# A hybrid decoder step: array divisions of the RWKV recurrence, 32x32 blocks in the GLA mixer, and decode states moved in halves

## The chip, the cores and the metric

The kernel runs on one core of one Trainium2 chip. The metric is the device time of one execution in microseconds (us), as the median of three runs. One more execution was taken by the hardware profiler. Its rows are what this document reads. The engines are called as in the profile: PE (matrix multiplications), DVE, ACT and POOL (elementwise work), SP (it issues the loads). POOL also issues the stores.

## What is computed

A trunk of four layers, each a mixer followed by an MLP with squared ReLU, works on 256 prompt tokens and 8 sampled tokens (one for each of 8 decode sequences). The tokens lie side by side as 264 columns, with the 1024 features in 8 groups of 128 partitions. The mixers are RWKV-7, GLA, a short convolution and a pooling. The change touches the first two.

```python
def step(S, inp):                       # RWKV-7, 16 heads of 64 values x 64 keys
    r_t, w_t, k_t, v_t, a_t, b_t = inp
    sa = einsum('bhvk,bhk->bhv', S, a_t)
    S = S * w_t[:, :, None, :] + sa[..., None] * b_t[:, :, None, :] + v_t[..., None] * k_t[:, :, None, :]
    return S, einsum('bhvk,bhk->bhv', S, r_t)

def step(S, inp):                       # GLA, 4 heads of 128 keys x 256 values
    qc, kc, vc, gc = inp
    b = cumsum(gc, axis=1)
    o_inter = einsum('bchk,bhkv->bchv', qc * exp(b), S)
    dec = exp(where(mask, b[:, :, None] - b[:, None, :], -inf))
    att = einsum('btshk,bthk,bshk->bhts', dec, qc, kc)
    o_intra = einsum('bhts,bshv->bthv', att, vc)
...
def sqrelu_mlp(x, w_up, w_down):
    return square(relu(x @ w_up)) @ w_down
```

Both mixers also update a state for each of the 8 decode sequences (`state_rwkv_wkv`, `state_gla`), which is loaded, used once and stored.

## The kernel before

**Stages.** The program runs the RWKV mixer, MLP 0, the GLA mixer, MLP 1, the convolution, MLP 2, the pooling and MLP 3. Weights come in tiles of 512 KB by SP's queue. In the RWKV mixer they are used as float32 (`wfull`, line 272; each float32 matmul stands as two records in the trace). Elsewhere they are split into a high and a low float32r part (`whi`, `wlo`, lines 180 and 188) and used in three matmuls (lines 232 to 234).

**Divisions of the array.** A matmul with 128 rows and 128 columns of weights uses the whole array. A matmul that reads 64 or 32 partitions, or writes 64 or 32, uses a part of it, and the array is divided accordingly (128x64, 64x64, 32x32 and so on, rows x columns). The profile prints a matmul's rows and columns, as in `64*64`.

**RWKV mixer.** The prompt is cut into 4 chunks of 64 tokens. Projections (`acc<-xm,wfull`) and three low-rank paths (`ps<-lo,wa`, `ps<-hw,wa`, the gate's `ps<-lx,g1a`, `ps<-lx,g1b`) come first. `keys` normalises the keys (`pss<-ksq,ph` sums squares per head into 8 rows, `pkk<-kc,gb` spreads the result from 8 rows back over 128). `pA` forms each chunk's products. A triangular solve on DVE (`zt`, `Zs`, 124 instructions) follows, ending in two transposes, `Zt` and `Wt`. Two rounds of `pQ` (32x32 blocks) complete the inverse. Then the recurrence over the chunks runs: `state_step` does `pU`, copies it to `Us`, does `pSA<-Us,MT`, copies that to `XV`, does `pS<-XV,BT` and updates `XV`. `output_step` does `pY<-rT,XV` and `pY<-AR,XV`. In `pSA` and in the first `pY` the two heads of a pair lie on the upper and the lower 64 partitions (64x64 division). In `pU`, `pS` and the second `pY` they lie on the left and right 64 columns (128x64 division). `rT` is the receptance times the decay, and `rb` a block form of it for `pAr`. `gate` does `pg<-hg,g2a` and `pg<-hg,gb`. `dacc<-yo,wfull` (line 1053) is the output projection.

**Decode of RWKV.** `decode` updates the states `wS` in four quarters of 512 KB. Each quarter is loaded in two halves (one per 64 partitions), and after the update both halves are stored, and the tile for the quarter after the next is loaded. These steps are advanced one at a time inside MLP 0.

**GLA mixer.** A prompt tile has 128 tokens. The attention matrix is built by levels: level n covers pairs of blocks of 64, 32, ..., 1 tokens, plus the diagonal. Levels 0 and 1 are small matmuls (line 1248). Levels 2 to 7 each take 4 whole 128x128 matmuls (line 1253, `gA<-gZQ,gEX`), and a masked copy of 128x512 (COPY_PREDICATED, line 1254) picks the few blocks that count. For decode, each state half `gSs` is split into a high and a low part (`gSq`, on ACT, DVE and POOL) and multiplied in float32r (line 1410, `gos<-gSq,gqz`, 128x32 division). `decode_update` (line 1396) then forms the new state.

**Order.** `RWKV_PLAN` and `GLA_PLAN` are written by hand. Each word is one step of a named piece of work. Tables (`RWKV_ENGINES`, `GLA_ENGINES`) give each copy or product its engine (V is DVE, A is ACT, G is POOL). Each engine runs its own instructions in order.

Of the kernel before, what the change touches and what calls it, by code (L numbers as in the profile page):

```python
# [450 lines left out]
def rwkv_early(k):  # L451
# [6 lines left out]
    for x in (hw, hg1, g1b, gb):  # L458
        nc.vector.memset(x, 0.0)
# [1313 lines left out]
```

## Time and profile before

| what | value |
|---|---|
| runs | 1316.86, 1316.26, 1315.95 us; median 1316.26 us |
| profiled execution | 1313.01 us, its span 1311.2 us |
| RWKV mixer | 0 to 256 us of the span |
| MLP 0 | 256 to 460 us |
| GLA mixer | 460 to 624 us |
| the rest | 624 to 1311 us |
| PE / DVE / ACT / POOL busy | 97% / 68% / 44% / 29% |
| mean granted clock of PE | 0.99 of full speed |

The span runs from the first to the last recorded instruction. The profiled execution lies 3.25 us below the median of the runs. PEclk is the granted clock in parts of 2.4 GHz, so 0.5 means 1.2 GHz. Busy time counts an instruction's own time; matmuls overlap in the pipeline, so the time from one start to the next is shorter than the mean duration of one.

### The profile page before, as it was taken

Reading aid. Unit: us, or ns where it says so; the run is one execution under the profiler, and the core shown is the slowest. Engines: PE = TensorE matmul, PEld = TensorE weight load, DVE = VectorE, ACT = ScalarE, POOL = GpSimd, SP = SyncE. Lnnn points to the kernel's source line nnn. Section 1 sums busy time; section 2 is a strip of 40 time slices with the busy share of each in tenths; the row PEclk is TensorE's granted clock in tenths of the full one; section 3 lists DMA queues with packets and bytes.
Section 4 is the critical chain, followed back from the end, with each engine's and each line's share of the span. In section 5 each row is a group of like instructions: output and inputs, shape, how many; then the busy total and the mean of one; then the engine's idle time right before and its main releaser. Section 6 shows DMA issues by size and latency. Waiting matters only on the chain.

```text
span 1311.2 us, 25583 instructions
## 1 busy us (share of the span) xinstructions
PE 1276.8 (97%) x10318; PEld 1224.9 (93%) x10318; DVE 897.5 (68%) x1398; ACT 571.4 (44%) x949; POOL 381.3 (29%) x415
## 2 busy tenths in 40 slices
PE   8999999999899998999999999999999999999997
PEld 7888787999899987899999999999999999999996
DVE  6467978697855579988766455877665556666443
ACT  2512343543434443346545344445444445444342
POOL 6133144243300227545333000332332002233000
PEclk9999989999999999999999999999999999999998
DMA  9333110467566542644655555555655673555552
GB/s 277 103 119 107 48 51 10 137 197 196 184 209 198 168 148 87 216 170 152 187 179 176 193 177 176 181 180 163 191 177 180 206 234 97 159 180 177 185 185 83
DMA packets 168024, 211.10 MB, mean 161 GB/s; under 512 B 11569, under 2 KB 125137, under 8 KB 167906
## 3 DMA queue, kind: packets, MB, share of 16 engines
q1 hardware_dynamic: 165122, 201.82, 48.8%
q0 software_dynamic: 2784, 7.65, 1.9%
q8 instruction: 81, 1.33, 0.4%
q14 instruction: 37, 0.30, 0.1%
HBM read 200.62 MB, written 8.82 MB: 160 GB/s over the span
## 4 chain that ended last, share of the span: by engine, by line
PE 83%; DVE 10%; DMA 2%; issue 2%; ACT 1%; POOL 0%; DVEq 0%; SPq 0%; ACTq 0%; POOLq 0%
PE acc L232 11%; PE acc L234 11%; PE acc L233 11%; PE dacc L234 11%; PE dacc L233 11%; PE dacc L232 11%; PE acc L272 5%; DMA wraw<-in_ffn_up 2%; PE dacc L1053 2%; DVE wlo L188 1%; PE pss L373 1%; DVE zt L736 1%; DVE Zs L738 1%; PE pQ L761 1%; PE gE L1215 0%
## 5 line engine op out<-in xcount | busy, mean ns | idle before, releaser
L188 DVE TENSOR_TENSOR wlo<-wraw,whi 128x1024 fp32r<-128x1024 f32 x310 | 390.8, 1263 | 227.8 <-ACT whi L180 226.9
L180 ACT CAST whi<-wraw 128x1024 fp32r<-128x1024 f32 x310 | 324.4, 1049 | 405.0 <-PE dacc L233 176.8
L232 PE MATMUL acc<-xh,whi 128*128 128x264 f32 x1408 | 397.0, 286 | 3.6 <-DVE ft L399 1.6
L234 PE MATMUL acc<-xh,wlo 128*128 128x264 f32 x1408 | 398.7, 286 | 1.8 <-DVE wlo L188 1.8
L233 PE MATMUL acc<-xl,whi 128*128 128x264 f32 x1408 | 398.9, 285 | 0.0
L233 PE MATMUL dacc<-sl,whi 128*128 128x264 f32 x1024 | 288.7, 284 | 0.0
L232 PE MATMUL dacc<-sh,whi 128*128 128x264 f32 x1024 | 287.8, 284 | 0.0
L234 PE MATMUL dacc<-sh,wlo 128*128 128x264 f32 x1024 | 283.8, 284 | 0.0
L232 PEld LDWEIGHTS acc<-xh,whi 128*128 128x128 f32 x1408 | 263.5, 189 | 6.6 <-DVE ft L399 2.2
L234 PEld LDWEIGHTS acc<-xh,wlo 128*128 128x128 f32 x1408 | 264.0, 188 | 4.8 <-DVE wlo L188 2.6
L233 PEld LDWEIGHTS acc<-xl,whi 128*128 128x128 f32 x1408 | 265.0, 188 | 0.5
L403 POOL TENSOR_TENSOR fs<-ft 128x264 f32<-128x264 f32 x128 | 133.0, 1042 | 252.3 <-DVE ft L399 250.9
L233 PEld LDWEIGHTS dacc<-sl,whi 128*128 128x128 f32 x1024 | 192.8, 188 | 0.0
L232 PEld LDWEIGHTS dacc<-sh,whi 128*128 128x128 f32 x1024 | 192.6, 188 | 0.0
L234 PEld LDWEIGHTS dacc<-sh,wlo 128*128 128x128 f32 x1024 | 189.7, 188 | 0.0
L346 POOL TENSOR_TENSOR sq<-sq 128x264 f32<-128x264 f32 x35 | 32.6, 932 | 361.1 <-ACT sq L342 360.6
L272 PE MATMUL acc<-xm,wfull 128*128 128x264 f32 x384 | 89.2, 388 | 0.2
L272 PEld LDWEIGHTS acc<-xm,wfull 128*128 128x128 f32 x384 | 72.0, 190 | 14.2 <-issue 1.2
L404 DVE TENSOR_TENSOR sl<-fs,sh 128x264 fp32r<-128x264 f32 x128 | 58.2, 472 | 25.0 <-POOL fs L403 25.0
L399 DVE SCALAR_TENSOR_TENSOR ft<-acc,rstd 128x264 f32<-128x264 f32 x96 | 40.9, 428 | 38.8 <-PE acc L234 38.6
L401 ACT ACTIVATE sh<-ft 128x264 fp32r<-128x264 f32 x128 | 50.9, 420 | 37.0 <-DVE ft L399 34.8
L342 ACT ACTIVATE sq<-hT 128x264 f32<-128x264 f32 x56 | 23.5, 419 | 37.8 <-DVE hT L383 35.5
(465 smaller groups left out, 1576.7 us busy)
## 6 DMA issues: line engine op xcount, KB each, us to landing
wraw<-in_ffn_up SPq DMA_DIRECT2D x128, 512.0 KB
wraw<-in_ffn_down SPq DMA_DIRECT2D x128, 512.0 KB
wraw<-in_gla_w_in SPq DMA_DIRECT2D x24, 512.0 KB
wraw<-in_conv_w_in SPq DMA_DIRECT2D x24, 512.0 KB
wfull<-in_rwkv_wk SPq DMA_DIRECT2D x8, 512.0 KB
wfull<-in_rwkv_wv SPq DMA_DIRECT2D x8, 512.0 KB
wS<-in_state_wkv SPq DMA_DIRECT2D x16, 256.0 KB
wfull<-in_rwkv_wr SPq DMA_DIRECT2D x8, 512.0 KB
```

The costliest lines, as they stand in the source:

```text
L180: return e.copy(out, x) if scale is None else e.activation(out, x, AF.Copy, scale=scale)
L188: return self.on(site, i).tensor_tensor(out, x, y, op=op)
L232: mm(acc, h, xh, start=first, stop=False)
L233: mm(acc, h, xl, start=False, stop=False)
L234: mm(acc, l, xh, start=False, stop=last)
L272: self.nc.tensor.matmul(accs[mi][:, :NT], w[:, kk, mi * 128:(mi + 1) * 128], self.at(X, k), start=(k == 0), stop=(k == 7))
L346: self.nc.gpsimd.tensor_tensor(ss[0], ss[0], sq, op=ALU.add)
L399: nc.vector.scalar_tensor_tensor(t, acc, 0.0, rs, op0=ALU.max, op1=ALU.mult)
L401: nc.scalar.activation(h, t, AF.Square)
L403: nc.gpsimd.tensor_tensor(s, t, t, op=ALU.mult)
L404: nc.vector.tensor_tensor(l, s, h.bitcast(F32), op=ALU.subtract)
L1053: mm(acc, wo[m][:, kk, :], at(Y, kk)[:, cs], start=(kk == 0), stop=(kk == 7))
```

## The change

Four things are done, and both plans and the engine tables are written anew.

1. RWKV recurrence: `Us` becomes two tiles padded with zeros, and `output_step` uses `rb` instead of `rT`, so that `pSA` and both `pY` have 128 rows and 64 columns, and alternate the left and right half. Four `rb` tiles are kept instead of two. `keys` uses four 32-column strips for `pss` and 32 rows for `pkk`. `pQ` alternates its two halves. The gate's second part has 32 rows in strips (`g2b`). DVE's memsets of `hg1`, `g1b` and `gb` at the start go.
2. RWKV decode: the halves of a quarter are stored and loaded in separate steps.
3. GLA levels 2 to 7: 32x32 blocks on the diagonal, each a matmul of 128 rows and 32 columns of weights. Three levels share a PSUM bank, and the masked copy is 128x128, into a tile `gin` that `placed` copies to `att`.
4. GLA decode: the splits into `gSq` go. `gos` is formed in float32, with four strips of 32 columns that each hold one of the four partial sums.

```diff
-    "AAVAGAAV", "mq": "VAAAVVVA", "v": "AAVVAVAA", "vec4": "AVVVAVGV", "rb": "AGAGGVVAAAAAAGVA", "vec5": "AVVAAAAV",
+    "AAVAGAAV", "mq": "AAAAVVVA", "v": "AAVVAVAA", "vec4": "AVVVAVGV", "rb": "VVVVVVVVVVVVVVVV", "vec5": "AVVAAAAV",
...
-        p, x, c = k.bank("pss")[0:8, :NT], k.t("kx", [8, NT]), k.t("kc", [8, NT])
+        p, x, c = k.bank("pss")[:, :NT], k.t("kx"), k.t("kc")
         for mi in range(4):
-            mm(p, sel[:, mi, 0:8], sq[:, mi], start=(mi == 0), stop=(mi == 3))
+            mm(p[mi * 32:(mi + 1) * 32], k.C("rsel")[:, 0:32], sq[:, mi], start=True, stop=True)
...
-            V.tensor_tensor(r, acc[:, :NP].rearrange("p (c t) -> p c t", c=4), dc, op=ALU.mult)
...
+        for par in range(2):
+            o = OWN[par]
+            k.product("rb", m * 2 + par, rb[m // 2][o, m % 2, :, par, :], acc[o, :NP].rearrange("p (c t) -> p c t", c=4), dc[o])
...
         for qv in range(4):
             S, vs, T = wS[qv], slice(qv * 16, (qv + 1) * 16), [k.slab([128, 16, 64], "wT") for _ in range(2)]
             op(T[0], vb(vt[:, 4, vs]), kb(3), ALU.mult)
+            if qv > 0:
+                store(qv - 1, 1)
             yield
             op(T[1], vb(sav[:, vs]), kb(2), ALU.mult)
+            if qv in (1, 2):
+                decode_load(qv + 1, (0,))
             yield
...
-            for h2 in range(2):
-                k.store(Sdst[h2][:, :, qv * 1024:(qv + 1) * 1024], S[OWN[h2]].rearrange("p v k -> p (v k)"))
-            if qv < 2:
-                decode_load(qv + 2)
+            store(qv, 0)
             yield
...
-        Us = k.t("Us", [128, 256])
-        k.put("us", c * 2 + a, Us, pU[:, :256])
+        for par in range(2):
+            o = OWN[par]
+            k.put("us", (c * 2 + a) * 2 + par, Us[par][o], pU[o, :256])
...
-                mm(p[o, mi * 64:(mi + 1) * 64], MT[un // 16][o, un % 16, :], Us[o, mi * 64:(mi + 1) * 64],
-                   start=True, stop=True)
+            for par in range(2):
+                mm(p[OWN[par], mi * 64:(mi + 1) * 64], MT[un // 16][:, un % 16, :], Us[par][:, mi * 64:(mi + 1) * 64],
+                   start=True, stop=True)
...
-        for hd in range(4):
-            a, b = (EX[t][hd][:, n, :], ZQ[t][hd][:, n, :]) if n < 7 else (kT[:, hd, tok], qT[:, hd, tok])
-            mm(p[:, hd * 128:(hd + 1) * 128], a, b, start=True, stop=True)
-        V.copy_predicated(att[t][:, :, 0:128], msk[:, n, :].unsqueeze(1).to_broadcast([128, 4, 128]),
-                          p.rearrange("p (h t) -> p h t", h=4))
+        lv = range(3 * n - 4, 3 * n - 1)
+        pv = p[:, 0:384].rearrange("p (l h t) -> p l h t", l=3, h=4)
+        for i, l in enumerate(lv):
+            for hd in range(4):
+                x, y = (EX[t][hd][:, l], ZQ[t][hd][:, l]) if l < 7 else (kT[:, hd, tok], qT[:, hd, tok])
+                for j in range(4):
+                    b = slice(j * 32, (j + 1) * 32)
+                    mm(pv[b, i, hd], x[:, b], y[:, b], start=True, stop=True)
+        for i, l in enumerate(lv):
+            V.copy_predicated(inner[t], msk[:, l - 2, :].unsqueeze(1).to_broadcast([128, 4, 32]), pv[:, i])
...
-        for h2 in range(2):
-            for i in range(2):
-                met[hp] += 1
-                mm(po[hp][0:32, h2 * 256:(h2 + 1) * 256], qz[:, (hp * 2 + h2) * NS + b, :], Sp[g, h][:, i, h2, :],
-                   start=(met[hp] == 1), stop=(met[hp] == 32))
+        met[hp] += 1
+        for h in range(2):
+            for h2 in range(2):
+                r = (h2 * 2 + h) * 32
+                mm(po[hp][r:r + 32, 0:256], qz[:, (hp * 2 + h2) * NS + of(g, h)[1], :], S[g][:, h, h2, :],
+                   start=(met[hp] == 1), stop=(met[hp] == 4))
```

How the rewritten plans move instructions is seen at three places. First, the start: PE's order right behind the sums for the low-rank paths (`acc<-xg,wad`), in the kernel before. `wa` is the second low-rank weight, `g1a` and `g1b` the gate's first.

```order
L497 MATMUL acc<-xg,wad 128x264 x8
L272 MATMUL acc<-xm,wfull 128x264 x21
L617 MATMUL ps<-lx,g1a 128x264
L618 MATMUL ps<-lx,g1b 128x264
L617 MATMUL ps<-lx,g1a 128x264
```

The same place in the changed kernel.

```order
L490 MATMUL acc<-xg,wad 128x264 x8
L591 MATMUL ps<-lo_142,wa_183 128x264 x2
L613 MATMUL ps<-lx,g1a 128x264 x6
L614 MATMUL ps<-lx,g1b 128x264
L582 MATMUL ps<-hw,wa_183 128x264
L614 MATMUL ps<-lx,g1b 128x264 x4
L582 MATMUL ps<-hw,wa_183 128x264 x2
L267 MATMUL acc<-xm,wfull 128x264 x5
```

The 21 projection matmuls that stood ahead of the gate now stand behind two low-rank paths and most of the gate. SP's loads behind that, before (`wa` is loaded in two halves, `wfull` tiles are 512 KB).

```order
L150 DMA g1b<-in_rwkv_g 128x8x32
L150 DMA gb<-in_spread 16x1024
L150 DMA gb<-in_rwkv_g 32x1024
L283 DMA wfull<-in_rwkv_wk 128x4x256 x5
L150 DMA wa_189<-in_rwkv_w 64x1024
L150 DMA wa_189<-in_rwkv_a 64x1024
L283 DMA wfull<-in_rwkv_wk 128x4x256 x2
L283 DMA wfull<-in_rwkv_wv 128x4x256 x2
L150 DMA g1a<-in_rwkv_g 128x8x128
```

And in the changed kernel.

```order
L278 DMA wfull<-in_rwkv_wk 128x4x256 x7
L278 DMA wfull<-in_rwkv_wv 128x4x256
L145 DMA wa_183<-in_rwkv_w 64x1024
L145 DMA wa_183<-in_rwkv_a 64x1024
L278 DMA wfull<-in_rwkv_wv 128x4x256
L145 DMA g1a<-in_rwkv_g 128x8x128
L145 DMA g1r<-in_rwkv_g 128x8x32
```

Eight large tiles instead of five now stand ahead of `wa`, and nine ahead of `g1a`, as before. Second, DVE right behind the second transpose of the solve, before.

```order
L743 STREAM_TRANSPOSE Wt<-Zs 128x32x32
L193 TENSOR_TENSOR bg<-pb,vT 128x264
L834 SCALAR_TENSOR_TENSOR bg<-bg,prm,pg 128x264
L184 TENSOR_SCALAR gT<-pg,prm 128x264
L182 COPY MT<-Wt 32x16x32 x2
L182 COPY Qs<-pQ 32x512
L193 TENSOR_TENSOR AR<-pAr,ph 128x256 x2
L193 TENSOR_TENSOR bg<-pb,vT 128x264
L834 SCALAR_TENSOR_TENSOR bg<-bg,prm,pg 128x264 x2
```

And in the changed kernel.

```order
L738 STREAM_TRANSPOSE Wt<-Zs 128x32x32
L177 COPY MT<-Wt 32x16x32 x2
L188 TENSOR_TENSOR AR<-pAr,ph 128x256 x2
L188 TENSOR_TENSOR bg<-pb,vT 128x264
L188 TENSOR_TENSOR AR<-pAr,ph 128x256 x2
L188 TENSOR_TENSOR bg<-pb,vT 128x264
L177 COPY MT<-pQ 32x16x32 x3
L188 TENSOR_TENSOR AR<-pAr,ph 128x256 x2
L188 TENSOR_TENSOR bg<-pb,vT 128x264
L836 SCALAR_TENSOR_TENSOR bg<-bg,prm,pg 128x264 x2
```

Eight `AR` products and four `bg` products now stand behind the transpose, where there were two and two; the rest stood in the solve, among its short instructions. Third, SP in MLP 0, before (`wraw` tiles are 512 KB of weights).

```order
L221 DMA wraw<-in_ffn_up 128x4x256 x15
L150 DMA wS<-in_state_wkv 64x1x1024 x2
L221 DMA wraw<-in_ffn_up 128x4x256 x9
L150 DMA wS<-in_state_wkv 64x1x1024 x2
L221 DMA wraw<-in_ffn_up 128x4x256 x8
```

And in the changed kernel.

```order
L216 DMA wraw<-in_ffn_up 128x4x256 x19
L145 DMA wS<-in_state_wkv 64x1x1024 x2
L216 DMA wraw<-in_ffn_up 128x4x256 x8
L145 DMA wS<-in_state_wkv 64x1x1024 x2
L216 DMA wraw<-in_ffn_up 128x4x256 x5
```

The two pairs of state loads come four and three weight tiles later, and each pair still stands together.

## Rows read from the trace of the kernel before

**Rows 1.** Windows: us, busy us of each engine (instructions), granted clock, DMA.

```profile
20.00:32.00 12.00, 11.85 (x52) 9.37 (x51) 7.78 (x17) 0.94 (x2) 11.98 (x20) 1.00 1.03 286
32.00:113.00 81.00, 81.00 (x379) 66.30 (x379) 47.86 (x91) 27.19 (x73) 24.83 (x34) 1.00 0.36 115
123.00:162.00 39.00, 36.87 (x226) 31.66 (x225) 37.03 (x106) 15.85 (x44) 6.15 (x11) 0.96 0.23 68
162.00:222.00 60.00, 55.73 (x944) 46.71 (x942) 51.56 (x84) 23.99 (x55) 28.32 (x28) 0.94 0.12 33
222.00:256.00 34.00, 33.72 (x276) 32.36 (x277) 22.25 (x63) 14.62 (x41) 7.11 (x14) 1.00 0.32 98
314.00:345.00 31.00, 27.19 (x210) 25.81 (x209) 23.82 (x32) 11.59 (x17) 8.93 (x11) 1.00 0.71 186
460.00:624.00 164.00, 154.99 (x1185) 143.98 (x1184) 143.37 (x218) 74.42 (x149) 86.42 (x69) 0.99 0.48 155
```

**Rows 2.** Timeline of PE at the start: start, us, line, operation.

```profile
17.84 3.81 PE L497 MATMUL acc<-xg,wad 128*128 128x264 f32 x16
21.49 10.20 PE L272 MATMUL acc<-xm,wfull 128*128 128x264 f32 x42
31.52 0.68 PE L617 MATMUL ps<-lx,g1a 128*128 128x264 f32 x2
```

**Rows 3.** Timeline of PE, key norms: sums of squares.

```profile
92.01 1.95 PE L665 MATMUL pss<-ksq,ph 128*8 128x264 f32 x8
```

**Rows 4.** Timeline of PE, key norms: spread over the heads.

```profile
101.65 2.04 PE L675 MATMUL pkk<-kc,gb 8*128 8x264 f32 x8
```

**Rows 5.** Timeline of PE, gate and second round of 32x32 blocks.

```profile
171.94 0.61 PE L833 MATMUL pg<-hg,gb 128*128 128x264 f32 x2
172.47 3.93 PE L761 MATMUL pQ<-Wt,Qs 32*32 32x32 f32 x128
```

**Rows 6.** Timeline of PE in one step of the recurrence.

```profile
209.26 0.69 PE L990 MATMUL pU<-XV,AKa 128*64 128x64 f32 x16
...
211.03 0.22 PE L1004 MATMUL pSA<-Us,MT 64*64 64x64 f32 x1
211.04 0.22 PE L1026 MATMUL pY<-rT,XV 64*64 64x64 f32 x1
...
211.15 1.58 PE L1004 MATMUL pSA<-Us,MT 64*64 64x64 f32 x29
```

**Rows 7.** Groups of DVE in the RWKV mixer: busy us, mean ns, idle before.

```profile
L193 DVE TENSOR_TENSOR AR<-pAr,ph 128x256 f32<-128x256 f32 x16 | 6.0, 415 | 0.0
...
L834 DVE SCALAR_TENSOR_TENSOR bg<-bg,prm,pg 128x264 f32<-128x264 f32 x8 | 3.9, 483 | 3.4 <-PE pg L833 3.4
...
L786 DVE TENSOR_TENSOR rT<-acc,Dc 128x256 f32<-128x256 f32 x7 | 2.9, 419 | 0.1
...
L182 DVE COPY rb<-rT 64x256 f32<-64x256 f32 x3 | 1.0, 324 | 0.0
```

**Rows 8.** Waits in MLP 0: total us, times, longest.

```profile
ACT whi L180 <- DMA wraw<-in_ffn_up: 9.2, 3, 5.9
```

**Rows 9.** Timeline of PE in the GLA levels, with idle time and releaser.

```profile
512.26 1.95 PE L1253 MATMUL gA<-gZQ,gEX 128*128 128x128 f32 x16
...
518.66 0.68 PE L1248 MATMUL gA<-gZQ,gEX 128*64 128x64 f32 x8 [1.54 <-DVE att L1254]
```

**Rows 10.** Timeline of PE: one group of the GLA decode output.

```profile
540.16 0.62 PE L1410 MATMUL gos<-gSq,gqz 128*32 128x256 f32 x4
540.62 0.40 PE L1393 MATMUL gkv<-gvs,gkm 128*128 128x256 f32 x2
```

**Rows 11.** Groups of DVE in the GLA mixer.

```profile
L188 DVE TENSOR_TENSOR gSq<-gSs,gSq 128x512 fp32r<-128x512 f32 x9 | 10.7, 1206 | 1.1 <-ACT gSq L180 1.1
...
L1254 DVE COPY_PREDICATED att<-gmask,gA 128x512 f32<-128x512 uint32 x12 | 8.7, 734 | 2.4 <-PE gA L1253 1.4 <-ACT att L180 0.6 <-PE gA L1248 0.5
...
L182 DVE CAST gSq<-gSs 128x512 fp32r<-128x512 f32 x4 | 3.9, 966 | 0.7 <-DMA gSs<-in_state_gla 0.7
```

More of the change, by code (lines that the diff above doesn't have):

```diff
@@ L455, in rwkv_early @@
     nc = k.nc
[L457 to L460 removed]
+    hw = k.t("hw")
+    nc.vector.memset(hw[64:128], 0.0)
+    k.zeroed = hw
     st = k.res.tile([128, 8, NS], F32, name="shst")
@@ L672, in keys @@
         yield
-        for mi in range(4):
-            p = k.bank("pkk")[:, :NT]
-            mm(p, spread[0:8, mi], c, start=True, stop=True)
-            V.scalar_tensor_tensor(kk[:, mi], kk[:, mi], 2.0 ** 10, p, op0=ALU.mult, op1=ALU.mult)
+        for mp in range(2):
+            ps = [k.bank("pkk")[:, :NT] for _ in range(2)]
+            for i in range(2):
+                q = slice((mp * 2 + i) * 32, (mp * 2 + i + 1) * 32)
+                mm(ps[i], k.C("rspr")[q], c[q], start=True, stop=True)
+            for i in range(2):
+                x = kk[:, mp * 2 + i]
+                V.scalar_tensor_tensor(x, x, 2.0 ** 10, ps[i], op0=ALU.mult, op1=ALU.mult)
         V.scalar_tensor_tensor(flat(aT[a]), flat(aT[a]), -1.0, flat(kk), op0=ALU.mult, op1=ALU.mult)
@@ L770, in ev_v @@
         k.put("vec4", m, vec[:, 4, m, :], at(vT, m)[:, NP:])
-    rT, bg = [k.slab([128, 4, 4, 64], "rT") for _ in range(2)], two("bg")
     rb = [k.slab([128, 2, 4, 2, 64], "rb") for _ in range(2)]
+    bg = two("bg")
+    rb += [k.slab([128, 2, 4, 2, 64], "rb") for _ in range(2)]
+    for x in rb:
+        G.memset(x, 0.0)
     for a in range(2):
-        G.memset(rb[a], 0.0)
         for cp in range(2):
@@ L904, in vb, with decode_load @@
         return x.unsqueeze(2).to_broadcast([128, 16, 64])
-    def decode_load(qv):
-        wS[qv] = k.slab([128, 16, 64], "wS")
-        for h2 in range(2):
+    def decode_load(qv, halves=(0, 1)):
+        if halves[0] == 0:
+            wS[qv] = k.slab([128, 16, 64], "wS")
+        for h2 in halves:
             k.load(wS[qv][OWN[h2]].rearrange("p v k -> p (v k)"), Ssrc[h2][:, :, qv * 1024:(qv + 1) * 1024])
@@ L983, in values @@
                 k.put("xv", (w * 2 + a) * 2 + par, XV[c][par][o, a * 4:(a + 1) * 4], pv[o, :, par, :].unsqueeze(2).to_broadcast([64, 4, 2, 64]))
+    pads = []
     def state_step(c, a):
+        if not pads:
+            pads.extend([k.t("Us", [128, 256]) for _ in range(2)] for _ in range(2))
+            for x in pads:
+                G.memset(x[0][HI], 0.0)
+                G.memset(x[1][LO], 0.0)
+        Us = pads[a]
         xv, ms = XV[c], slice(a * 4, a * 4 + 4)
@@ L1237, in gla_layer @@
         G.memset(x, 0.0)
+    inner = [k.t("gin", [128, 4, 32]) for _ in range(2)]
+    for x in inner:
+        G.memset(x, 0.0)
     def attend(t, n):
@@ L1329, in decode_gate @@
         G.tensor_tensor(pick[0:24], pick[0:24], eye[0:24, 16:24], op=ALU.add)
[L1330 to L1334 removed]
+        qp = qz.rearrange("p (h b) j -> p h (b j)", h=4)
+        G.tensor_tensor(qp[:, :, 0:256:33], qT[:, :, ST], e, op=ALU.mult)
     ks, vs = k.slab([128, 512], "gks", F32R), k.slab([128, 1024], "gvs", F32R)
@@ L1420, in decode_done1 @@
         pv = p[:, 0:64].rearrange("p (h v b) -> p h v b", h=4, v=2)
-        for hd in range(4):
+        for hp in range(2):
             for vt in range(2):
-                mm(pv[:, hd, vt], sd[hd][:, vt * 128:(vt + 1) * 128], k.C("eye16")[0:16, 96:104], start=True, stop=True)
+                mm(pv[:, 2 * hp:2 * hp + 2, vt], sd[hp][:, vt * 128:(vt + 1) * 128],
+                   k.C("eye16")[:, 96:112].rearrange("p (h b) -> p h b", h=2), start=True, stop=True)
         V.tensor_tensor(o, pv, sv, op=ALU.add)
```

168 lines of the change are left out of this document (82 added, 86 removed), and 23 rows, old and new, of tables (GLA_ENGINES, GLA_PLAN).

## The prediction, on record before the changed kernel ran

> **What bounds the kernel now.** I read the windows by stage first. From 32 to 113 us PE is busy in every microsecond, and from 20 to 32 us it is short of 0.15 us only while the DMA engines are full (1.03) [rows 1]: loads and PE together bound the beginning. In the solve (123 to 162) DVE is busy 37.0 of 39 us, so DVE bounds it. From 162 to 222, the recurrence, DVE has 51.6 of 60 us and PE 55.7, with the clock granted at 0.94: neither is full, and they wait for each other in a chain. From 222 on PE has it again. In MLP 0 the stretch from 314 to 345 has 3.8 us of idle PE [rows 1], and in it ACT's casts waited 9.2 us for weights [rows 8]. In the GLA mixer PE is busy 155.0 of 164 us and DVE 143.4 [rows 1]: PE bounds it, but DVE is so full that PE waits for it, as for the masked copy of one level, 1.54 us [rows 9]. The reader is to see that the same saving on PE is worth its full size before 113 us and after 460 us, and little between 123 and 222 us.
>
> **The start.** Behind the `wad` sums, which end at 21.5 us, PE now runs 21 projection matmuls until 31.5, when `g1a` is there [rows 2]. In the changed order two `wa` matmuls and the gate stand there. `wa` comes behind three more tiles of 512 KB (1.5 MB at 286 GB/s [rows 1] are 5.5 us), and `g1a` behind as many tiles as before, with 0.33 MB of small loads fewer ahead of it, so some 1.1 us earlier, near 30.4. By 31.5 PE has then done about four matmuls of 2 x 0.223 us (0.223 is the start-to-start time of a record, (1.95 - 0.39) / 7 [rows 3]), 1.9 us in place of 9.4. I take 7.5 us lost. Bounds: 4, if the loads run faster without the small ones, and 10.3, if the gap also brings a stretch of half clock (2.8 us more, the order of the 0.06 x 60 = 3.6 us that the recurrence loses to it [rows 1]).
>
> **Until the last `pA`.** Seven projections fewer stand before it: 7 x 0.446 = -3.1. `pss` is two groups of 8 records at 0.223, 3.6 us [rows 3]. In four column strips it would take a quarter if the strips run side by side. Two halves do: 16 records of `pU`, alternating, come every (0.69 - 0.22) / 15 = 31 ns, while `pSA`, mostly on one half, takes (1.58 - 0.22) / 28 = 49 ns, and records of two divisions start 10 ns apart [rows 6]. I take -2.3 (0 to -2.7). `pkk`, two groups of 8 at (2.04 - 0.39) / 7 = 0.236 [rows 4], halves: -1.6 (0 to -1.9). With the start: +0.5.
>
> **The solve.** On DVE 14 `rb` products come in (64x256, priced like `AR`, 0.42 us: 5.9), 5 `rT` (0.42) and 3 `rb` copies (0.32) go, and 6 `AR` (0.42), 3 `bg` with `pg` (0.48) and 2 other `bg` (like `AR`) move behind the transpose [rows 7]: 5.9 - 2.1 - 1.0 - 2.5 - 1.4 - 0.8 = -1.9, and about +0.4 of small ones. DVE bounds, so -1.5.
>
> **The recurrence.** What moved out of the solve comes in here: 4.7 us. To it come six normalisation products that stood later (6 x 0.42 = 2.5), and 8 half copies of `Us` for 3 whole ones (5 x 0.42 = 2.1). The `ya` copies, now whole, are 3 fewer (-1.3), and the other moved copies are about +0.7. The sum is +8.7 us on DVE. It had 8.4 us idle [rows 1], so it could just hold them if all its waits could be filled; but they lie in a chain with PE. I take half: +4, between 0.3 and 8.7. PE saves 3 x 128 records x (49 - 31) ns = 6.9 us [rows 6], which only adds to its idle time. The 16 second parts of the gate now change the division: the record before `pQ` shows 0.53 us for two records of 0.223, so 0.09 for a change [rows 5], 1.5 us, also idle time of PE. Work of 2.5 us that moved ahead shortens the tail, where PE bounds: -1 (0 to -2.5).
>
> First mixer: 0.5 - 1.5 + 4 - 1 = **+2**.
>
> **MLP 0.** The state loads come later by four and three weight tiles and the steps lie apart, so the 9.2 us of waiting for weights [rows 8] should shrink. The pairs still stand together on SP. I take -2.5 of the 3.8 us (0 to -3.8).
>
> **GLA on PE.** The decode output: 64 records at (0.62 - 0.28) / 3 = 0.113, 7.3 us [rows 10], become 64 records of 0.223 x 256 / 264 = 0.216 us in four strips. Side by side that is 3.5 us, one after another 13.8. I take -3.8 (up to +6.5), nearest to the two halves of [rows 6]. The levels: 96 records at (1.95 - 0.28) / 15 = 0.111, 10.7 us [rows 9], become 384 records. The 32x32 blocks of `pQ` come every (3.93 - 0.19) / 127 = 29.4 ns [rows 5], which gives 11.3 us. No row shows a stream faster than that, so I take +0.6; four strips at a quarter would give 2.8, -7.9. Levels 0 and 1 alternate strips, -0.8, four fewer small decode matmuls of two records -0.9. Some 16 changes of division go, at 0.09: -1.5. Sum -6.4.
>
> The Trainium skill, page "TensorE: Matmul & The Clock Gate", section "Back-to-back issue gap", speaks against this change: a short matmul is bound by its issue, by some 25 ns, or 62 ns where the sequencer decodes it in software. By an estimate from the latter the 192 matmuls of the levels would take 11.9 us, +1.2 in place of +0.6. The rows lie close to it: 2 x 29.4 ns for `pQ`, 2 x 31 ns for `pU` [rows 5, 6]. The page "TensorEngine Tiling (Array Packing)", section "Key Properties", lets tiles of the array work in parallel, which for the decode output gives the 3.5 us taken above; for four strips no row shows it.
>
> **GLA waits.** DVE loses 9 subtractions (10.7 us), 4 casts (3.9) and 12 masked copies of 734 ns (8.7) [rows 11]. The new copies have a quarter of the columns, between 0.18 and 0.73 us each; at 0.3 they are 3.6. That is -19.7 us of 143.4. PE's 9.0 us of idle time [rows 1] should shrink by some 3 (0 to 6). GLA: **-9.4**.
>
> **Sum.** 2 - 2.5 - 9.4 = -9.9 us. The profiled execution of 1313.0 us (span 1311.2 and 1.8 around it) would become 1303.1. It lies 3.25 us under the median, so the runs should show 1306.4. A difference of 0.2%, 2.6 us, is about what a measurement of this kernel can tell from none.
>
> **Rivals.**
> *PE's saving counts in full in the first mixer.* DVE holds the added work (+0.3 for +4), the start loses 4, the tail gives 2.5 and the keys all: -7 there, 1297.4. For it: DVE's 8.4 us of idle time. Against it: the chain.
> *DVE is the bound from the solve to the end of the mixer.* It holds none of the 8.7 us, the solve gains nothing, and the tail gives nothing: +0.5 + 8.7 = +9.2, so 1313.6. For it: 37.0 of 39 us and 51.6 of 60 are busy already.
> *The strips run one after another.* The decode output takes 13.8 us (+6.5 for -3.8), the keys gain nothing (+3.9), levels 0 and 1 nothing (+0.8): 15 us worse, 1321.4, slower than before. It decides where a strip's record costs over about 0.15 us in the decode output with the keys ungained. Against it: two halves do overlap.
> *MLP 0 keeps its stall*, since loads and stores move as many bytes in pairs: 1308.9.
>
> **How the numbers follow.** Forecast 0.42 (own range 1300 to 1312); PE's saving in full 0.12; DVE bound 0.18; strips in series 0.15; stall stays 0.13. Faster: 0.40 + 0.12 + 0.08 + 0.10 = 0.70. Same: 0.02 + 0.06 + 0.04 + 0.02 = 0.14. Slower: 0.04 + 0.11 + 0.01 = 0.16. The range from 1297 to 1320 leaves out the better part of the strips in series and a little below.
>
> **What would show it.** In the changed profile: PE idle between 21.5 and 30 us and at the same work some 7 us late; the last `pA` near its old time; DVE over 95% busy between the transposes and the first `dacc`; `dacc` 2 to 4 us later; less idle PE in MLP 0; `gos` records every 54 ns, level records every 29 ns, and DVE below 130 us in GLA. The prediction fails if the gap at the start stays small, if DVE's work in the recurrence stretches the chain by its whole size, or if strips don't overlap.

## The result, and the profile after

| what | before | changed kernel |
|---|---|---|
| median of the runs | 1316.56 us (4 runs, 1315.95 to 1317.95) | 1293.17 us (4 runs, 1292.43 to 1293.61) |
| profiled execution, its span | 1313.01, 1311.2 us | 1292.43, 1290.6 us |

The ratio is 0.9832 [0.9816, 0.9847]: 1.7% faster, 23.4 us. The forecast of 1306.4 us had the direction right and less than half of the size, and the time lies 3.8 us below the range. In the profiled executions the difference is 20.6 us. The rest, 2.8 us, is that the profiled execution of before lay 3.5 us under its median, and that of the changed kernel 0.7.

Where the time went is read from the starts of the same work on PE in the two timelines.

| place | before | after | shift |
|---|---|---|---|
| first `pA` | 81.2 | 88.2 | +6.9 |
| last `pA` | 117.1 | 115.4 | -1.7 |
| first `pQ` | 162.5 | 160.7 | -1.8 |
| first `dacc` of the RWKV mixer | 222.0 | 225.8 | +3.9 |
| MLP 0, first matmul | 256.4 | 260.6 | +4.2 |
| MLP 0, first `dacc` | 358.6 | 354.6 | -4.0 |
| GLA, first `dacc` | 593.9 | 573.7 | -20.2 |
| end of the span | 1311.2 | 1290.6 | -20.6 |

So the first mixer lost 4.2 us (forecast +2), MLP 0 gained 8.2 up to its first `dacc` (forecast 2.5), the way from there to GLA's first `dacc` gained 16.2 (forecast 9.4) and the rest 0.4.

First the windows of the changed kernel by stage, with the columns of [rows 1].

```profile
21.30:38.00 16.70, 10.81 (x35) 8.26 (x35) 8.53 (x17) 3.79 (x8) 13.87 (x18) 0.80 0.67 166
38.00:116.00 78.00, 78.00 (x404) 65.44 (x403) 50.08 (x99) 27.27 (x78) 24.82 (x32) 1.00 0.31 102
...
315.60:341.20 25.60, 25.60 (x211) 25.40 (x210) 23.79 (x31) 11.94 (x17) 9.99 (x11) 1.00 0.78 222
...
456.00:604.00 148.00, 140.62 (x1469) 129.10 (x1467) 129.88 (x202) 72.20 (x146) 80.43 (x58) 1.00 0.52 172
```

PE now has a hole at the start (5.9 us idle of 16.7, and a mean clock of 0.80), none any more in the hard stretch of MLP 0, and 14.4 us less work in GLA than in [rows 1].

The hole at the start, in PE's timeline. It answers to [rows 2].

```profile
17.58 3.81 PE L490 MATMUL acc<-xg,wad 128*128 128x264 f32 x16
26.27 1.82 PE L591 MATMUL ps<-lo,wa 128*128 128x264 f32 x4 [4.88 <-POOL lo L577]
29.09 5.08 PE L613 MATMUL ps<-lx,g1a 128*128 128x264 f32 x12 [1.00 <-DMA g1a<-in_rwkv_g]
```

And POOL's timeline there.

```profile
22.20 1.28 POOL L179 TENSOR_SCALAR lx<-du,prm 128x264 f32<-128x264 f32 x1
23.40 2.56 POOL L552 TENSOR_TENSOR lx<-lx,u 128x264 f32<-128x264 f32 x3
25.91 0.31 POOL L577 MEMSET lo<- 64x264 f32 x1
26.17 3.62 POOL L774 MEMSET rb<- 128x1024 f32 x4
```

PE waits 4.88 us for a memset of 0.31 us that stands on POOL behind 3.8 us of the gate's inputs (1.28 and 2.56), and only 1.00 us for a load. Behind the hole the clock is at the lower of its two levels, 1.2 GHz (0.50), for 6.83 us.

```profile
26.62:33.45 6.83, 5.83 (x14) 4.06 (x13) 2.47 (x7) 2.20 (x4) 6.67 (x9) 0.50 0.73 203
```

In this stretch PE is busy for 5.83 us and does about half as much as at 2.4 GHz (14 records, 0.42 us each, where [rows 3] has one every 0.223), so some 2.9 us of work are lost.

The key norms, in PE's timeline, answer to [rows 3, 4]: 1.95 and 2.04 us have become 0.66 and 0.73.

```profile
91.81 0.66 PE L656 MATMUL pss<-ksq,ph 128*32 128x264 f32 x8
...
101.05 0.73 PE L668 MATMUL pkk<-kc,ph 32*128 32x264 f32 x8
```

The solve, from the last `pA` to the first `pQ`: windows of before, then of the changed kernel.

```profile
117.10:162.50 45.40, 43.27 (x271) 36.63 (x269) 42.55 (x119) 18.16 (x54) 6.49 (x12) 0.96 0.24 70
```

```profile
115.40:160.70 45.30, 38.01 (x241) 32.24 (x240) 42.81 (x116) 12.36 (x37) 7.45 (x14) 0.99 0.32 94
```

It takes as long as before, and DVE has as much work in it. The recurrence, from the first `pQ` to `dacc`, in the same order.

```profile
162.50:222.00 59.50, 55.23 (x942) 46.61 (x941) 51.06 (x83) 23.99 (x55) 28.32 (x28) 0.94 0.13 33
```

```profile
160.70:225.80 65.10, 58.80 (x996) 45.83 (x996) 52.07 (x96) 26.33 (x61) 27.39 (x26) 0.93 0.10 26
```

It is 5.6 us longer, but DVE has only 1.0 us more work in it, and PE 3.6 us more. The groups of PE in the same stretches say which work that is, before first.

```profile
L1030 PE MATMUL pY<-AR,XV 128*64 128x64 f32 x128 | 9.5, 225 | 0.0
L1026 PE MATMUL pY<-rT,XV 64*64 64x64 f32 x128 | 9.2, 224 | 1.1 <-DVE gn L865 1.1
...
L832 PE MATMUL pg<-hg,g2a 128*128 128x264 f32 x8 | 3.5, 530 | 0.0
L833 PE MATMUL pg<-hg,gb 128*128 128x264 f32 x9 | 3.4, 457 | 0.0
...
L802 PE MATMUL pAr<-rb,BK 128*128 128x128 f32 x8 | 1.5, 347 | 0.0
```

Changed kernel:

```profile
L1052 PE MATMUL pY<-AR,XV 128*64 128x64 f32 x128 | 7.5, 236 | 0.0
...
L1049 PE MATMUL pY<-rb,XV 128*64 128x64 f32 x128 | 7.0, 241 | 3.4 <-DVE gnr L357 3.0 <-DVE XV L177 0.2
...
L834 PE MATMUL pg<-hg,g2b 32*128 32x264 f32 x16 | 5.7, 433 | 0.0
L798 PE MATMUL pAr<-rb,BK 128*128 128x128 f32 x32 | 5.4, 323 | 0.0
L832 PE MATMUL pg<-hg,g2a 128*128 128x264 f32 x16 | 5.4, 419 | 0.0
```

The two `pY` save 4.2 us, but `pg` and `pAr` that stood in the solve before now bring 8.1 (11.1 for 6.9, and 5.4 for 1.5).

MLP 0: its waits from 303 to 345 us, as [rows 8] (9.2 us from 314 to 345), and the windows from 256 to 345 us, before and after.

```profile
ACT whi L175 <- DMA wraw<-in_ffn_up: 4.1, 4, 2.5
```

```profile
256.00:345.00 89.00, 84.14 (x669) 82.09 (x669) 75.36 (x102) 39.44 (x60) 30.17 (x31) 1.00 0.67 188
```

```profile
256.00:345.00 89.00, 88.23 (x727) 87.83 (x726) 79.87 (x108) 43.48 (x66) 32.03 (x33) 1.00 0.67 201
```

Read the counts, not the busy time: 669 records before and 727 after. Later in MLP 0, where the kernel before has no stall, the row is this:

```profile
345.00:400.00 55.00, 55.00 (x454) 55.00 (x453) 37.02 (x40) 22.65 (x27) 9.24 (x12) 1.00 0.63 203
```

So a record takes 0.121 us from start to start. At this rate 669 records need 81 us, so PE lost 8 of 89 us, of which it shows 4.9 as idle.

GLA: the levels and the decode output in PE's timeline, answering to [rows 9, 10].

```profile
509.15 0.28 PE L228 MATMUL acc<-xl,whi 128*128 128x264 f32 x1
509.27 0.28 PE L229 MATMUL acc<-xh,wlo 128*128 128x264 f32 x1
509.49 1.03 PE L1285 MATMUL gA<-gZQ,gEX 128*32 128x32 f32 x96
...
516.79 0.20 PE L1285 MATMUL gA<-gZQ,gEX 128*32 128x32 f32 x1
...
518.09 0.64 PE L1442 MATMUL gos<-gSs,gqz 128*32 128x256 f32 x8
...
536.43 1.07 PE L1442 MATMUL gos<-gSs,gqz 128*32 128x256 f32 x16
```

The 96 records of three levels take 1.03 us, so they start every (1.03 - 0.20) / 95 = 8.7 ns (0.20 is one record alone), and the other three groups take 1.03 to 1.11 us; 29.4 ns were forecast. The records of `gos` come every (1.07 - 0.64) / 8 = 54 ns, as forecast. The groups of PE in GLA, before and after:

```profile
L1253 PE MATMUL gA<-gZQ,gEX 128*128 128x128 f32 x80 | 10.5, 276 | 0.0
L1410 PE MATMUL gos<-gSq,gqz 128*32 128x256 f32 x64 | 10.4, 287 | 1.8 <-DVE gSq L182 0.9 <-DVE gSq L188 0.8
...
L1253 PE MATMUL gA<-qT,kT 128*128 128x128 f32 x16 | 2.2, 281 | 0.0
```

```profile
L1442 PE MATMUL gos<-gSs,gqz 128*32 128x256 f32 x64 | 4.5, 386 | 0.0
L1285 PE MATMUL gA<-gZQ,gEX 128*32 128x32 f32 x320 | 3.6, 199 | 0.0
...
L1285 PE MATMUL gA<-qT,kT 128*32 128x32 f32 x64 | 1.0, 201 | 0.0
```

The levels went from 12.7 to 4.6 us of PE, the decode output from 10.4 to 4.5. On DVE the masked copy of [rows 11] has become 296 ns, where 0.3 us was forecast.

```profile
L1287 DVE COPY_PREDICATED gin<-gmask,gA 128x128 f32<-128x128 uint32 x12 | 3.6, 296 | 0.2
```

### The profile page after: what moved, and what is told of

Its sections match the earlier page's. It is cut to its first block, busy times and chain, and to the rows that moved or that the text cites. A ratio compares the mean times of both kernels' runs of the same rounds, so it can differ in the third digit from the quotient of the medians.

```text
span 1290.6 us, 26064 instructions
## 1 busy us (share of the span) xinstructions
PE 1249.4 (97%) x10598; PEld 1196.6 (93%) x10598; DVE 880.9 (68%) x1389; ACT 566.7 (44%) x935; POOL 375.3 (29%) x407
## 4 chain that ended last, share of the span: by engine, by line
PE 86%; DVE 9%; DMA 2%; issue 1%; SPq 1%; ACT 1%; POOL 0%; DVEq 0%; POOLq 0%; ACTq 0%
PE acc L227 13%; PE acc L228 13%; PE acc L229 13%; PE dacc L229 11%; PE dacc L228 11%; PE dacc L227 11%; PE acc L267 4%; PE dacc L1074 2%; DMA g1a<-in_rwkv_g 1%; DVE zt L731 1%; DVE Zs L733 1%; PE pss L368 1%; DMA wS<-in_state_wkv 0%; DVE gZQ L183 0%; PE pQ L757 0%
```

## The experiments

All are variants of the changed kernel. Each ratio is to the kernel before, run beside it. "Against the changed kernel" is the difference of the two ratios (0.9832 for the changed kernel) times 1316.56 us. Medians are of 4 runs. Each interval is that of the ratio alone; that of the changed kernel, some 2 us to either side, comes on top of it in every difference.

The profiled executions tell more, stage by stage, because most variants leave most stages as they are. The same work then shows how far one execution differs from another:

| stretch | before | executions in which it is as in the changed kernel |
|---|---|---|
| span's start to the last `pA` | 117.1 us | 113.5 to 115.9 us (9 executions) |
| second round of `pQ` to the first `dacc` | 49.5 | 55.5 to 57.2 (9) |
| first matmul to the first `dacc` of MLP 0 | 102.2 | 93.7 to 96.0 (11) |
| first `dacc` of MLP 0 to that of GLA | 235.3 | 219.0 to 219.5 (10) |

A variant differs in a stretch, beyond the scatter, where it leaves the range.

**levels_whole** forms levels 2 to 7 with whole 128x128 matmuls and masked copies of 128x512 again.

```diff
-                for j in range(4):
-                    b = slice(j * 32, (j + 1) * 32)
-                    mm(pv[b, i, hd], x[:, b], y[:, b], start=True, stop=True)
+                mm(p[:, hd * 128:(hd + 1) * 128], x, y, start=True, stop=True)
+            V.copy_predicated(att[t][:, :, 0:128], msk[:, l, :].unsqueeze(1).to_broadcast([128, 4, 128]),
+                              p.rearrange("p (h t) -> p h t", h=4))
```

> The changed kernel, with GLA levels 2 to 7 as before: four whole 128x128 matmuls and a masked copy of 128x512 each, straight into att. Theory (the strips of the levels are what was under-priced: 384 records at 8.7 ns against 96 at 111 ns, 7.4 us of PE, and 5 us of DVE): 7 to 12 us slower than the changed kernel, about 1302. Rival (the saving in GLA came from dropping the splits of the decode states, and the levels hide beside DVE): at most 3 us slower, under 1297.

Measured: 1304.22 us, 0.9904 [0.9882, 0.9925], 9.5 us above the changed kernel. GLA's first `dacc` comes at 584.6 us instead of 573.7, and from MLP 0's first `dacc` to it are 228.9 us, 9.8 more than the changed kernel's 219.1. In the groups of DVE the copies are long again:

```profile
L1284 DVE COPY_PREDICATED att<-gmask,gA 128x512 f32<-128x512 uint32 x12 | 8.8, 731 | 2.0 <-PE gA L1283 1.7
```

So the levels' part of the change is worth some 9.5 us of the 16.2, on PE, DVE and in waits together, where its term for PE was +0.6. No run puts the decode output back by itself, so its share of the rest is read from busy times alone.

**levels_same_strip** issues the four heads of a strip behind one another (8 records of one strip, then the next strip). **strip_by_strip** issues all 24 records of a strip, with the three levels in the inner loop. Neither changes DVE's instructions.

```diff
         for i, l in enumerate(lv):
-            for hd in range(4):
-                x, y = (EX[t][hd][:, l], ZQ[t][hd][:, l]) if l < 7 else (kT[:, hd, tok], qT[:, hd, tok])
-                for j in range(4):
+            for j in range(4):
+                for hd in range(4):
+                    x, y = (EX[t][hd][:, l], ZQ[t][hd][:, l]) if l < 7 else (kT[:, hd, tok], qT[:, hd, tok])
```

> The changed kernel, with the 16 matmuls of a level in another order: all four heads of a strip in a row, where the strips alternated from matmul to matmul. Theory (records come every 8.7 ns because neighbours lie in different strips; in one strip they come every 29 ns as pQ did): the four groups of 96 records take 2.8 us each in place of 0.9, the kernel is 5 to 8 us slower than the changed one, about 1299. Rival (a short record costs its issue alone, whatever strip): the groups keep 0.9 us and the time stays within 1.5 us.

```diff
-        for i, l in enumerate(lv):
-            for hd in range(4):
...
-                for j in range(4):
...
+        for j in range(4):
...
+            for i, l in enumerate(lv):
+                for hd in range(4):
...
```

> The changed kernel with the 48 matmuls of three GLA levels in the order of the strips: 24 records of one strip in a row, where levels_same_strip had 8 and the changed kernel alternates. Theory (neighbours in one strip follow each other at 26 to 29 ns, and overlap only where the strip changes): a group of 96 records takes 2.5 to 2.8 us, 0.9 with alternating strips and 2.0 with runs of 8; the kernel is 4 to 7 us slower than the changed one. Rival (PE looks ahead and fills the strips itself): near the 2.0 us of the runs of 8.

Measured: levels_same_strip 1294.85 us, 0.9836 [0.9818, 0.9854] (+0.5); strip_by_strip 1298.14 us, 0.9873 [0.985, 0.9895] (+5.4). One group of 96 records in PE's timeline of each of the two:

```profile
531.60 2.10 PE L1285 MATMUL gA<-gZQ,gEX 128*32 128x32 f32 x96
```

```profile
533.29 2.90 PE L1285 MATMUL gA<-gZQ,gEX 128*32 128x32 f32 x96
```

In one strip a record starts every (2.90 - 0.20) / 95 = 28.4 ns, as `pQ` did in [rows 5]; in groups of 8 every 20 ns; with neighbours in four strips every 8.7. So the order of issue decides, not the size of a matmul. The middle order costs 1.0 to 1.1 us more in each of the four groups. As a time of the whole kernel, +0.5 is inconclusive: the interval of the ratio alone reaches from -1.8 to +2.9. The stage shows it: from MLP 0's first `dacc` to GLA's are 221.3 us with the middle order, 2.2 more than in the changed kernel, and 224.9 with strip_by_strip, 5.8 more. So of the 4.3 and 7.4 us more that the four groups take on PE, about a half and three quarters reach the end of the stage.

**mlp0_pairs** puts the decode states' halves back into one step, stores and loads. **stores_paired** does it for the stores alone.

```diff
-            if qv in (1, 2):
-                decode_load(qv + 1, (0,))
...
-            store(qv, 0)
+            for h2 in range(2):
+                k.store(Sdst[h2][:, :, qv * 1024:(qv + 1) * 1024], S[OWN[h2]].rearrange("p v k -> p (v k)"))
+            if qv < 2:
+                decode_load(qv + 2)
```

> The changed kernel, with the RWKV decode update in MLP 0 as before: both halves of a quarter are stored together, and the tile after the next is loaded at once. Theory (the stalls of MLP 0 are bound to where these loads stand in SP's queue, and were 8 us, more than the idle time of PE in the windows showed): about 8 us slower than the changed kernel, 1301, and PE idle again between 313 and 340 us. Rival (the stalls went because of the other changes, such as the shift of the whole mixer against the loads): at most 2 us slower, under 1296.

```diff
-            if qv > 0:
-                store(qv - 1, 1)
...
             store(qv, 0)
+            store(qv, 1)
```

> The changed kernel with both halves of a decode quarter stored together after its update, and the loads as in the changed kernel. Theory (the stalls of MLP 0 come from the place of the state loads in SP's queue, which here stays late): within 1.5 us of the changed kernel. Rival (two stores at once with the loads are what held the weights up): 3 to 6 us slower, as with both put back.

Measured: mlp0_pairs 1297.02 us, 0.9857 [0.9841, 0.9872] (+3.3, the intervals overlap by little); stores_paired 1292.96 us, 0.9833 [0.9808, 0.9858] (+0.1). In the profiled execution of mlp0_pairs MLP 0 takes 100.1 us from its first matmul to its first `dacc`, 6.1 more than in the changed kernel and outside the range of the table: its matmuls run 1.2 us ahead of the changed kernel's when it begins, because the first mixer was shorter by as much, and 5.0 behind at the first `dacc`. stores_paired takes 95.6, inside the range. The window and the wait in mlp0_pairs:

```profile
315.00:345.00 30.00, 26.94 (x209) 25.47 (x208) 24.27 (x32) 11.75 (x18) 7.86 (x11) 1.00 0.69 196
```

```profile
ACT whi L175 <- DMA wraw<-in_ffn_up: 12.8, 7, 4.1
```

The 209 records in 30 us and the 12.8 us of ACT (from 300 to 345 us, where before has 10.0 and the changed kernel 4.1) are the stall of before [rows 1, 8]. The stores in pairs alone don't bring it back; with the loads at their old place too it is back. Whether the loads count because they come earlier or because they stand right behind the stores was not told apart, and no run has the loads at the old place with the stores apart.

**loads_first** issues the loads of `wa`, `g1a` and the gate's rest ahead of all tiles.

```diff
+    wa2 = k.slab([128, 1024], "wa2")
+    k.load(wa2[0:64, :], I["rwkv_w2"])
+    k.load(wa2[64:128, :], I["rwkv_a2"])
+    g1a = k.slab([128, 8, 128], "g1a")
+    k.load(g1a, g1v[:, :, 0:128])
```

> The changed kernel, with the loads of the second low-rank weight and of the gate's first weight moved ahead of the projection weights in SP's queue. Theory (the changed kernel loses 6 us of idle PE between 21.5 and 38 us, and 3 us more at half clock, and PE bounds until the last pA): 4 to 8 us faster than the changed kernel, about 1287. Rival (the solve on DVE, or the wait for projection weights that now come later, gives it back): within 2 us of it, 1291 to 1295.

Measured: 1304.49 us, 0.9908 [0.9888, 0.9928] (+10.0). Neither the theory nor the rival had this. PE's timeline:

```profile
31.80 2.13 PE L599 MATMUL ps<-lo,wa 128*128 128x264 f32 x4 [8.28 <-POOL lo L585]
```

With `wa` loaded ahead of all tiles PE waits 8.28 us: the memset of `lo` now stands behind the four `rb` memsets and five products on POOL and runs at 31.4. So the early load of `wa`, which the prediction named, doesn't free the start. Only a part of the +10.0 is explained by it: the last `pA` comes 6.0 us later than in the changed kernel, and the solve takes 3.7 more (49.0 us for 45.3), for a reason that stays open.

**projections_first** puts the projections ahead of the low-rank paths and the gate again.

```diff
-G R e a x0 R l0 x1 a X X X X X X h z z z X X x2 z a h z z a x3 h x4 k0 k1 a h a k1 h k0 h k1 a h k1 a z z R t k0 d5
...
+X X X X X X X X G R e x0 R l0 k0 k0 a a x1 h a h z h z a h z x2 h z a k1 h z a k1 h z x3 x4 h z a k1 a k1 z R t k0 d5
...
+            if m == 0:
+                k.queue_after(i, k.last_full)
```

> The changed kernel with the start in the order of the kernel before: PE runs 24 projection matmuls right behind the low-rank sums, and DVE makes their operands first (by the words of the plan and two issue orders). Theory (PE, which stood 5 us for a POOL memset behind the gate's products and 1 us for a load, and then ran 3 us at half clock, is the bound until the last pA): 4 to 8 us faster than the changed kernel, about 1287. Rival (DVE's solve sets the end of this part, so the idle time of PE at the start cost nothing): within 2 us of the changed kernel.

Measured: 1289.17 us, 0.9802 [0.9778, 0.9825] (-3.9), the fastest of all, though its interval overlaps with the changed kernel's. PE's timeline:

```profile
21.56 9.51 PE L267 MATMUL acc<-xm,wfull 128*128 128x264 f32 x42
33.91 2.64 PE L267 MATMUL acc<-xm,wfull 128*128 128x264 f32 x6 [2.84 <-POOL xm L552]
```

The last `pA` comes at 110.9, 4.5 us earlier than in the changed kernel and 2.7 below the range of the table, and of the 4.5 us 3.2 remain at the first `dacc`. A smaller wait for POOL is left.

**start_on_dve** is projections_first with the products and the memset that PE waited for moved from POOL (two of them from ACT) to DVE. **xv_on_act** moves the copies into `XV` from DVE to ACT, with the changed kernel's order. **start_and_xv** does both.

```diff
-    "u": "VV", "du": "VG", "mix0": "VAGVVAVV", "mix2": "VVVVVVVG", "mix3": "VVVVVVVV", "mix5": "VVVAGAVV", "hi0":
+    "u": "VV", "du": "VG", "mix0": "VAGVVAVV", "mix2": "VVVVVVVV", "mix3": "VVVVVVVV", "mix5": "VVVVVVVV", "hi0":
...
-        G.memset(low[0][LO, :], 0.0)
+        V.memset(low[0][LO, :], 0.0)
```

> projections_first, with the operand products of the keys and of the gate, and the memset of the low-rank operand, all on DVE instead of partly on POOL and ACT. Theory (there PE still waited 2.84 us for a product on POOL, behind 3.6 us of memsets, and ran at half clock after it): 1 to 3 us faster than projections_first, about 1287. Rival (DVE is late instead): within 1 us.

```diff
-    "xv": "AVAAAAAAVVAVAVVVAVVV", "us": "AVAVAVAVAVAVAVAV", "evr": "VVVVVVAV", "ar": "VVVVVVVVVVVVVVVV", "bgx":
+    "xv": "AAAAAAAAAAAAAAAAAAAA", "us": "AVAVAVAVAVAVAVAV", "evr": "VVVVVVAV", "ar": "VVVVVVVVVVVVVVVV", "bgx":
```

> The changed kernel with the seven copies of the values into the recurrence's operand that DVE did (64x512, 0.68 us each, 4.8 us) on ACT, which is busy 26 of 65 us there. Theory (DVE bounds the recurrence as a whole, which is why moving the gate moved only its start): 2 to 5 us faster than the changed kernel. Rival (a chain of PE, copy and update bounds it, with each engine waiting for the next): within 1 us, or slower where a copy on ACT delays the Us copies.

> start_on_dve and xv_on_act together. If the two are independent their differences add up: about 1284. If the recurrence is a chain, as start_on_dve.

Measured: start_on_dve 1292.74 us, 0.983 [0.9808, 0.9852] (-0.3). PE's hole is gone (busy 17.64 of 18 us from 20 to 38, at full clock), but the last `pA` stands at 110.6, where it stood in projections_first. The trace shows why: PE stands again, for another product of POOL, ahead of the first `pA`, and then runs at half clock.

```profile
77.62 3.03 PE L705 MATMUL pA<-AKa,BK 128*128 128x128 f32 x16 [2.09 <-POOL BK L183]
```

```profile
78.49:81.90 3.41, 3.41 (x15) 3.10 (x14) 2.87 (x6) 0.52 (x2) 2.76 (x3) 0.50 0.33 106
```

These 2.1 us and 1.7 us of lost work (half of 3.41) take the place of the hole of projections_first. The stretch from `dacc` to MLP 0 is longer too (37.6 us for 34.8; it has 310 records for 280, and 3.4 us of it are at half clock). xv_on_act 1290.58 us, 0.9812 [0.9792, 0.9833] (-2.6, intervals overlap; 1.5 us of it already stand at the last `pA`, ahead of the recurrence). From the second round of `pQ` to `dacc`, the changed kernel first, then xv_on_act:

```profile
168.68:225.84 57.16, 50.84 (x845) 38.35 (x845) 47.48 (x88) 20.58 (x51) 25.31 (x23) 0.97 0.12 30
```

```profile
168.44:225.10 56.66, 51.55 (x845) 39.09 (x845) 42.58 (x80) 25.09 (x59) 25.17 (x23) 0.94 0.12 30
```

DVE has 4.9 us less work, and the stretch is 0.5 us shorter, which is within the scatter: DVE's share in the chain is small. start_and_xv 1292.71 us, 0.9833 [0.9809, 0.9857] (+0.1): the two do not add up.

**no_alternation** issues in `pSA` and both `pY` all matmuls of one half, and then all of the other.

```diff
-        for mi in range(4):
-            un = (a * 4 + mi) * 4 + c
-            for par in range(2):
+        for par in range(2):
+            for mi in range(4):
+                un = (a * 4 + mi) * 4 + c
...
```

> The changed kernel with the two halves of the recurrence's matmuls one after the other in pSA and both pY (four records of one half in a row) instead of alternating. PE needs up to 7 us more for them. Theory (PE's saving in the recurrence fell into idle time and was worth nothing): within 1.5 us of the changed kernel. Rival (PE's part stands in the chain from Us to XV): 3 to 7 us slower.

Measured: 1295.95 us, 0.9855 [0.983, 0.988] (+3.0, intervals overlap). The same stretch, from the second round of `pQ` to `dacc`:

```profile
168.16:227.71 59.55, 53.92 (x847) 41.87 (x846) 47.83 (x90) 21.93 (x53) 23.95 (x25) 1.00 0.12 31
```

PE's busy time is up by 3.1 us (from 50.84), and the stretch by 2.4 (57.2 to 59.6), outside the range of the table. PE's work stands in the chain, against the prediction.

**gate_in_recurrence** moves three quarters of the gate from ahead of the first `pSA` to between its steps.

```diff
-T100 r2 b2 T001 r3 s r3 w01 s s b4 r3 r3 b7 T010 s b5 g3 b6 g0 T011 T110 g2 y1 S00 w21 T111 S01 S01 w30 S00 S01 S00
...
+b2 T001 r3 s r3 w01 s s b4 r3 r3 b7 T010 s b5 b6 T011 T110 y1 S00 w21 T111 S01 S01 w30 S00 g3 S01 S00 T101 S11 D0 l1
+w20 S10 g0 w31 S11 S10 S11 g2 O0 O0 D0 S10 S21 D1 l2 w41 S21 S20 O1 D2 w40 S21 D1 S20 l3 D2 S20 O1 S31 g1 S30 O2 D3
```

> The changed kernel with three of the gate's four steps moved in the plan from before the recurrence into its first steps. Theory (PE is busy 170 to 184 us with the gate, whose products stand on DVE and ACT ahead of the first Us copies, and so the recurrence starts 8 us later after pQ than before; inside the recurrence PE has idle time for it): pSA starts 5 us earlier, the kernel is 3 to 6 us faster. Rival (DVE is the bound of the whole stretch, and the same products cost the same later): within 2 us.

Measured: 1294.07 us, 0.9844 [0.9815, 0.9872] (+1.6, not resolved). PE's timeline:

```profile
176.41 0.30 PE L1024 MATMUL pSA<-Us,MT 128*64 128x64 f32 x2 [0.35 <-ACT Us L175]
```

The first `pSA` is 7.1 us earlier (183.55 in the changed kernel), the last at 221.0 instead of 221.4, and `dacc` at 226.7, later by 0.8. The same work of PE in another order ends at about the same time.

## Why the prediction was wrong

From 1306.4 to 1293.2 us it is -13.2: GLA -6.8, MLP 0 -5.7, first mixer +2.2, the rest -0.4, and -2.5 because before's profiled execution lay 3.25 us under the median then shown and the changed kernel's lies 0.7 under its own. By terms, in us (found, from the starts and groups above):

| term | forecast | found |
|---|---|---|
| the start | +7.5 | +8.6 |
| projections that moved behind the last `pA` | -3.1 | -4.5 |
| key norms, `pss` and `pkk` | -2.3, -1.6 | -2.6, -2.6 |
| solve | -1.5 | -0.1 |
| recurrence | +4 | +5.6 |
| tail | -1 | +0.3 |
| MLP 0 | -2.5 | -8.2 |
| GLA, levels 2 to 7 on PE | +0.6 | -8.1 |
| GLA, decode output on PE | -3.8 | -5.9 |
| GLA, everything else | -6.2 | -2.2 |

**The levels, the largest miss.** The step that failed is the term of +0.6 for levels 2 to 7, as 384 records every 29.4 ns. The mechanism, short matmuls in four strips, was the right one, and the prediction's alternative of -7.9 was what came: 384 x 8.7 ns is 3.3 us in place of 10.7, -7.4, and -8.1 by the groups' busy time. The price was taken from a row whose neighbours all lie in the same 32x32 block, and "No row shows a stream faster than that" was read as a limit, although [rows 6] had shown that records of different divisions start 10 ns apart. strip_by_strip gives nearly the forecast rate (28.4 ns) and 5.4 us. The page "TensorE: Matmul & The Clock Gate" of the Trainium skill, section "Back-to-back issue gap", gives a short matmul a floor of 25 ns from start to start, or 62 ns where it is decoded in software. One strip lies between the two (2 x 28.4 = 57 ns for a float32 matmul of two records), and four strips go below both (17 ns); the measurement decides. For four strips the page "TensorEngine Tiling (Array Packing)" of the Trainium skill, section "Key Properties", is borne out where it says that different tiles can work in parallel.

**The decode output** was priced by starts; its busy time fell by 5.9 us (10.4 to 4.5). Before, it ran mostly in short groups that also paid for their begin and end, and the new groups have 8 or 16 records. The rival in which strips run one behind another falls: 54 ns is a quarter of the 216 of one strip, so four strips of wide matmuls do run side by side. PE's idle time in GLA shrank by 1.6 us (9.0 to 7.4), where 3 was taken, and DVE's work by 13.5 (143.4 to 129.9), where 19.7 was. That the missing 6 cost little, with PE busy 140.6 of 148 us, is argued and not tested. No row shows by itself the 1.5 us for changes of division that go.

**MLP 0.** The step "-2.5 of the 3.8 us" bounded the gain by PE's idle time. That bound was wrong. Records of 0.28 us start 0.121 us apart, so a delay of up to some 0.16 us between two starts leaves no idle time. By counts, the 210 records of [rows 1] from 314 to 345 need 25.4 of 31 us, 5.6 lost, and 8 over the whole 256 to 345. The changed kernel does 211 records in 25.6 us. From MLP 0's first matmul to its first `dacc` 102.2 us became 94.0, so all 8 came back; mlp0_pairs takes 6.1 of them away again.

**The first mixer, the start.** The size was near, but the cause, late loads, is not what the trace shows. PE stands 5.7 us longer than before between 21.3 us and the last `pA`, 4.88 of them for POOL's queue and 1.00 for a load, and the half clock behind the hole costs 2.9 us of work, together 8.6. The prediction's sum leaves POOL's queue out. loads_first shows it by missing. The projections gave more than was taken, since 20 records moved behind the last `pA` (286 to 266) where 14 were counted, and so did the keys (2 x 1.29 and 2 x 1.31). Until the last `pA` it was -1.7 for +0.5; 0.6 of the -1.7 is in none of these terms.

**The solve** gained 0.1 us for 1.5. DVE's work in it was to fall and did not (42.6 to 42.8 us).

**The recurrence.** +4 was near the 5.6 found, for the wrong reason. DVE got 1.0 us more, not 8.7. The parts counted from the solve did come, but two products that were slow in before took 4.4 us less (`XV<-XV,dcl` 3.4 to 1.3 us for three, one `yo<-gn,bg` 2.9 to 0.7), and of the 2.5 us of normalisation products only 0.7 did. PE's saving, forecast at 6.9 and found in `pY`, `pSA` and `pQ` (about 6), was more than used up by `pg`, `pAr`, `pb` and `pbt`, which came in from the solve with the products that the prediction did move. It counted those products' DVE time and not the matmuls that feed them. That PE's work counts in this stretch and DVE's hardly is what no_alternation (+2.4 for +3.1) and xv_on_act (-0.5 for -4.9) show, each in one profiled execution, the first outside and the second inside a scatter of 1.7 us; how the chain splits in general stays open, and no run puts the old division of `pSA` and `pY` back.

Of the rivals, strips in series and the MLP 0 stall that stays did not come. DVE as the bound to the end of the mixer is refuted for the recurrence by xv_on_act. PE's saving in full, the nearest in time (1297.4), is not what happened either: the first mixer got longer, and the gain lies in MLP 0 and GLA. That the forecast of the first mixer (+2) and what came (+4.2) lie close is luck in part, since the start and the recurrence were near for other reasons and the solve and the tail missed.
